# Two padded small tiles, an earlier use of the first weight tile's low parts, and two sums of squares moved to VectorE in a streaming-encoder block

## The chip, the cores and the metric

One core of one Trainium2 chip runs the whole program. The metric is the device time of one execution in microseconds; the kernel before took 2420.36 us (median of 3 runs, 2420.31 to 2421.14).

## What is computed

One layer of a streaming encoder on x of 256 tokens by 2048 features, float32, with norm(x) = x * rsqrt(mean(x*x) + eps) * gain:

```python
x = x + 0.5 * swiglu(norm(x), ffn1_w_up, ffn1_w_down)      # 2048 -> 2 x 5632 -> 2048
proj = norm(x) @ w_in                                      # HGRN2, RG-LRU, gates
merged = g[..., 0, :] * (y_a @ w_branch_a) + g[..., 1, :] * (y_b @ w_branch_b)
x = x + merged @ w_out
x = x + cross_attention(norm(x), norm(mem), wq, wkv, wo)   # 4 heads, 256 memory tokens
x = x + 0.5 * swiglu(norm(x), ffn2_w_up, ffn2_w_down)
return norm(x)                                             # with the final gain
```

## The kernel before, in words

All matrices are float32, and TensorE multiplies in fp32r. Each operand is therefore split: ScalarE copies it to fp32r (its high part, `h` of a weight, `xh` of an activation; L156), and VectorE subtracts that from the original (its low part, `l` or `xl`; L157). A product is the sum of three matmuls: high by high, activation-low by weight-high (both L582), and activation-high by weight-low (L584). The weight is the moving operand, 128 x 512; the activation is the stationary one, 128 x 128.

A weight tile is 128 x 2048, 1 MB, in four quarters of 512 columns. `weights` keeps two tiles ahead of TensorE; `prepare` loads one (SyncE, L290 and others) and splits it. In the two feed-forward layers (`ffn`) a tile of the up-projection meets two operand halves and two token halves. A "plain" tile makes eight products of three matmuls each, 24 matmuls. A "fast" tile makes seven (a Winograd form): it needs sums of its quarters, made by VectorE in `td` (L314 to L317) and split to `th` and `tl`, so its low parts lie in two tiles: three of its seven weight-low matmuls read `l`, four read `tl`. A "mixed" tile uses differences of activations, `xd`, as stationary operands. The tables `FIRST` and `ffn_order` give 70 fast and 10 mixed tiles to the first feed-forward layer (FFN1), 86 and 2 to the second (FFN2). In FFN1, GpSimd's queue also makes some weight-low parts by an accumulating DMA.

Where tiles lie: pools opened for the whole program come first (`const`, `raw` 3 buffers, `h` 3, `l` 3, `slots` 22, then `small`). The pools of a stage (`scope`: `wide`, `xd`, `raw1`, `raw2`, `hd`, `tmp` and others) follow `small`. In the built program every buffer of `raw`, `h`, `l` and `slots` begins at 128 modulo 256 in its partition, and every buffer of a stage's pools at 0 modulo 256 (the first at 185088). `tl` lies in `wide`, a stage's pool. `xd` lies in a stage's pool in FFN1, and in `slots` in FFN2.

At the start, before the first eight tiles are in, the order on SyncE, ScalarE and VectorE is that of the code (`manual_schedule`): tile 0 comes in four quarters, `head_x` loads and splits the activations, and after tiles 4 and 5 `head_residual` loads the residual and adds up its squares for the first norm (`TokenSquares.add`, L468: one ScalarE instruction and a read of its accumulator for each of 4 column blocks c and 2 token halves). The results are first needed where FFN1's first group is activated. `three` writes the matmuls of a tile; TensorE's order is that of the code where the scheduler has no reason to differ.

Of the kernel before, what the change touches and what calls it, by code (L numbers as in the profile page):

```python
# [13 lines left out]
P = 128  # L14
# [80 lines left out]
def block_kernel(ctx: ExitStack, tc: tile.TileContext, xT, xin, memT, vec, gfin, bgate, lruw, wu1, wd1, win, wv,  # L95
# [362 lines left out]
    class TokenSquares:  # L458
# [2 lines left out]
        def __init__(self):  # L461
            self.ss = small.tile([P, 8 + PAD], F32, name="sst", tag="sst")[:, :8]

        def add(self, c, ts=range(2)):
            for t in ts:
                name = "hd" if "hd" in scoped else "tmp2"
                junk = scoped[name].tile([P, 512], F32, name="junk", tag=name)
                act.activation(junk, xt[c][:, t * 512:(t + 1) * 512], ACT.Square,  # L468
                               accum_out=self.ss[:, t * 4 + c:t * 4 + c + 1])

        def rstd_tokens(self, ts=range(2)):
            std = small.tile([P, 2], F32, name="stdt", tag="stdt")
# [99 lines left out]

    held = []

    def three(products, last=0, hold=False, apart=0):


        high = [(acc, ah, bh, start) for acc, (ah, al), (bh, bl), start, _ in products]
        low = [(acc, al, bh, False) for acc, (ah, al), (bh, bl), _, _ in products]
        for i in range(len(high) + apart):  # L580
            for acc, a, b, start in high[i:i + 1] + (low[i - apart:i - apart + 1] if i >= apart else []):
                pe.matmul(acc, a, b, start=start, stop=False)  # L582
        for acc, (ah, al), (bh, bl), _, stop in held + products[last:] + ([] if hold else products[:last]):
            pe.matmul(acc, ah, bl, start=False, stop=stop)  # L584
        held[:] = products[:last] if hold else []
# [13 lines left out]
    def ffn(name, pairs, sq, then, begin=(), sums=()):  # L599
# [38 lines left out]
        for at, e in enumerate(order):  # L638
            w = weights(name, *e)
            kind = e[0]  # L640
            following = order[at + 1][0] if at + 1 < len(order) else None
            if kind != "down":
                g, p = e[1:]
                fast = kind == "fast"
                products = []
                for i, (a, b, n) in enumerate(PRODUCTS["ready" if sums_ready(name, e) else kind]):
                    u = uses[g, n]
                    if u[0] == (p, i):
                        accs[n] = bank()
                    own, less = pairs[p]  # L650
                    products.append((accs[n], part(own, a, P) if a >= 0 else part(less, -1 - a, P), part(w[b // 4] if fast else w, b % 4, 512),
                                     u[0] == (p, i), u[-1] == (p, i)))
                three(products, 3 if adds(name, e) else 0, adds(name, e) and p == 6,
                      2 if at == 0 and name == "ffn1" else 0)
                last = at + 1 == len(order) or order[at + 1][1] != g or following == "down"
                ends = kind != "plain" and uses[g, 0][-1][0] == p
                if ends or last:
                    if ends or kind == "plain":
                        if "hid" in scoped:
                            ev = [scoped[n].tile([P, 1024], F32, name=n, tag=n) for n in ("hid", "hd")]  # L660
                            e0, e3, e1, e2 = (v[:, i:i + 512] for v in ev for i in (0, 512))
                        else:
                            ev = scoped["wide"].tile([P, 2048], F32, name="ev", tag="wide")
                            e0, e1, e2, e3 = (ev[:, i * 512:(i + 1) * 512] for i in range(4))
                        if rstd is None:
                            with tc.issue_after(done["high"]):
                                rstd = sq.rstd_tokens()
                if ends:
                    act.activation(e0, accs[0], ACT.Copy)
                    dve.tensor_tensor(out=e1, in0=accs[5], in1=e0, op=ALU.add)  # L670
                    dve.tensor_tensor(out=e2, in0=accs[4], in1=e1, op=ALU.add)
                if last:
                    if kind == "plain":
                        activate(e0, accs[0], accs[1], 0)
                        activate(e3, accs[3], accs[2], 1)
                    else:
                        for o, n, x in ((e0, 1, e0), (e1, 3, e1), (e1, 2, e1)):
                            dve.tensor_tensor(out=o, in0=accs[n], in1=x, op=ALU.add)
                        activate(e0, e0, e1, 0)
                        for o, n, x in ((e3, 6, e2), (e2, 3, e2)):  # L680
                            dve.tensor_tensor(out=o, in0=accs[n], in1=x, op=ALU.add)
                        activate(e3, e3, e2, 1)
                    late.append((4 if g else 2, lambda g=g, hid=(e0, e3): turn(g, hid)))
            else:
                first, n, c, block = e[1:]
                if block == first:
                    accs["down"] = [bank(), bank()]
                for t in range(2):
                    products = []
                    for k in range(4):  # L690
                        a = hids[2 * block + k // 2][:, k % 2 * 512:][:, :512]
                        products.append((accs["down"][t], (a[:, t * P:][:, :P], a[:, T + t * P:][:, :P]),
                                         part(w, k, 512), block == first and k == 0, block == first + n - 1 and k == 3))
                    three(products)
                    if block == first + n - 1:
                        o = xt[c][:, t * 512:(t + 1) * 512]
                        done["residual"] = dve.scalar_tensor_tensor(out=o, in0=accs["down"][t], scalar=0.5, in1=o,
                                                                    op0=ALU.mult, op1=ALU.add).ins
                        if block == NG - 1:
                            then(c, t)  # L700
            if sums:
                sums.pop(0)()
            if begin:
                begin.pop(0)()
            tick()
# [36 lines left out]
    def head_residual(i):  # L742
        for c in (2 * i, 2 * i + 1):
            for t in range(2):
                sp.dma_start(xt[c][:, t * 512:(t + 1) * 512], xin[t * P:(t + 1) * P, c * 512:(c + 1) * 512])
            sq1.add(c)
        if i:
            sp.dma_start(vt[:, small_n:NVEC], vec[:, small_n:])

# [528 lines left out]
    def to_out(c, t):  # L1278
        if c % 2 == t == 0:
            gains.append(slot(name="gfin"))  # L1280
            sp.dma_start(gains[-1], gfin[:, c * 512:c * 512 + 1024])
        g = gains[c // 2][:, c % 2 * 512:][:, :512]
        sq5.add(c, [t])
        if c == 2:
            b = more.setdefault(t, small.tile([P, 2], F32, name=f"more{t}", tag=f"more{t}"))
            dve.tensor_reduce(out=b[:, :1], in_=sq5.ss[:, 4 * t:4 * t + 3], axis=mybir.AxisListType.X, op=ALU.add)
            dve.tensor_scalar(out=b[:, 1:], in0=b[:, :1], scalar1=1.0 / D, scalar2=EPS, op0=ALU.mult, op1=ALU.add)
        y = [xt[i][:, t * 512:(t + 1) * 512] for i in range(4)]
        if c < 3:
            dve.tensor_tensor(out=y[c], in0=y[c], in1=g, op=ALU.mult)  # L1290
        if c == 2 and t:
            root_ready(y[c])
        if c == 3:
            st = small.tile([P, 2], F32, name="stdt", tag="stdt")
            r = st[:, 1:]
            scaled = slot(name="scaled")[:, :512]
            dve.tensor_tensor(out=scaled, in0=y[3], in1=g, op=ALU.mult)
            act.activation(st[:, :1], sq5.ss[:, 4 * t + 3:4 * t + 4], ACT.Sqrt, bias=more[t][:, 1:], scale=1.0 / D)
            dve.reciprocal(out=r, in_=st[:, :1])
            if t:  # L1300
                with tc.issue_after(done["residual"]):
                    flush(put_off)

            def scale(i, o):
                if i > 1:
                    dve.tensor_scalar(out=o, in0=o, scalar1=r, scalar2=None, op0=ALU.mult)
                else:
                    act.activation(o, o, ACT.Copy, scale=r)
                sp.dma_start(out_[t * P:(t + 1) * P, i * 512:(i + 1) * 512], o)

            for i, o in ((3, scaled), (0, y[0]), (2, y[2]), (1, y[1])):
                if t or i != 2:
                    scale(i, o)
                else:
                    put_off.append(lambda: scale(2, y[2]))
# [101 lines left out]
```

## Time and profile before

| | |
|---|---|
| median of 3 runs | 2420.36 us |
| the profiled execution | 2419.32 us, its span 2417.6 us |
| TensorE matmul busy | 2405.3 us (99%), clock 0.999 |
| VectorE / ScalarE busy | 2048.9 us (85%) / 1467.1 us (61%) |
| DMA | 684.34 MB, mean 283 GB/s |

Rows of the profile give an engine, a line, an operation, the tiles (out<-in), the shape and a count. A row of the timeline begins with its start and its length in microseconds; consecutive instructions of one kind are merged, with their count after the x. The length of a matmul (0.39 us) is not its share of the time: matmuls overlap, and what one costs is the distance from its start to the next one's start, here 0.226 to 0.24 us. FFN1 runs from 6 to about 690 us, FFN2 from about 1735 us to the end.

### The profile page before, as it was taken

To read this page: it belongs to the slowest core of one execution; us is meant where nothing else is said; L and a number is where in the kernel's file an instruction comes from. 1 tells how busy PE (TensorE), PEld (TensorE's weight loads), DVE (VectorE), ACT (ScalarE), POOL (GpSimd) and SP (SyncE) were. 2 spreads that over 40 slices of the span, in tenths; PEclk is the share of its full clock that TensorE was granted. 3 is DMA by queue.
4 is the path that set the end of the run, shared out by engine and by line. 5 is a ranking of instruction groups with operands and counts; after the bars stand their busy time and mean duration, and the time that the engine had idled before them with its cause. 6 is when DMAs were issued, how large, how long until landed. Compare 5 with 4: busy or idle time off the path is not lost.

```text
span 2417.6 us, 30836 instructions
## 1 busy us (share of the span) xinstructions
PE 2405.3 (99%) x12102; PEld 2002.6 (83%) x12102; DVE 2048.9 (85%) x2289; ACT 1467.1 (61%) x1506; POOL 102.3 (4%) x166
## 2 busy tenths in 40 slices
PE   9999999999999999999999999999999999999998
PEld 7888888888888888888888888888888788888887
DVE  7999999999876878688876777777789999999995
ACT  8566777777654454476434555455676666666664
POOL 0000000000000000000000000000000000000000
PEclk9999999999999999999999999999999999999999
DMA  8578999999858776878998899876787878777873
GB/s 306 202 224 257 277 275 274 271 276 276 270 211 316 275 286 247 301 280 315 356 330 338 304 356 337 325 294 239 266 340 304 293 272 288 268 285 275 293 279 142
DMA packets 102386, 684.34 MB, mean 283 GB/s; under 512 B 11360, under 2 KB 11616, under 8 KB 29280
## 3 DMA queue, kind: packets, MB, share of 16 engines
q1 hardware_dynamic: 78912, 519.82, 57.6%
q0 software_dynamic: 23328, 162.54, 22.4%
q8 instruction: 95, 1.56, 0.2%
q14 instruction: 51, 0.42, 0.0%
HBM read 619.40 MB, written 62.91 MB: 282 GB/s over the span
## 4 chain that ended last, share of the span: by engine, by line
PE 96%; ACT 2%; DMA 1%; DVE 1%; issue 0%; SPq 0%; ACTq 0%; DVEq 0%
PE acc L582 35%; PE acc L584 17%; PE acc L342 11%; PE acc L367 8%; PE acc L368 8%; PE acc L370 8%; PE acc L345 6%; ACT h L156 1%; PE acc L622 1%; PE acc L506 1%; DMA raw<-wu 1%; DVE l L157 0%; PE acc L938 0%; DMA raw<-wd 0%; PE acc L1237 0%
## 5 line engine op out<-in xcount | busy, mean ns | idle before, releaser
L156 ACT ACTIVATE h<-raw 128x2048 fp32r<-128x2048 f32 (+3 forms) x577 | 866.8, 1528 | 622.5 <-PE acc L368 211.4
L157 DVE TENSOR_TENSOR l<-raw,h 128x2048 fp32r<-128x2048 f32 (+2 forms) x405 | 833.0, 2059 | 211.4 <-ACT h L156 207.6
L582 PE MATMUL acc<-h,xh 128*128 128x512 f32 x1228 | 478.8, 393 | 2.0 <-ACT h L156 1.1
L582 PE MATMUL acc<-h,xl 128*128 128x512 f32 x1228 | 476.3, 390 | 0.0
L582 PE MATMUL acc<-h,hidop 128*128 128x512 f32 x1408 | 352.8, 391 | 1.4 <-ACT h L156 1.3
L367 PE MATMUL acc<-h,ops 128*128 128x512 f32 x832 | 326.3, 392 | 0.0
L368 PE MATMUL acc<-h,ops 128*128 128x512 f32 x832 | 324.4, 390 | 0.0
L582 PEld LDWEIGHTS acc<-h,hidop 128*128 128x128 f32 x1408 | 262.4, 188 | 56.7 <-ACT h L156 2.5
L582 PEld LDWEIGHTS acc<-h,xh 128*128 128x128 f32 x1228 | 230.3, 188 | 58.9 <-ACT h L156 7.5
L342 PE MATMUL acc<-ops,h 128*128 128x512 f32 x1152 | 277.5, 392 | 0.0
L582 PEld LDWEIGHTS acc<-h,xl 128*128 128x128 f32 x1228 | 230.6, 188 | 48.0
L342 PEld LDWEIGHTS acc<-ops,h 128*128 128x128 f32 x1152 | 211.4, 188 | 41.3
L157 DVE TENSOR_TENSOR tl<-raw,h 128x1024 fp32r<-128x1024 f32 x172 | 203.6, 1218 | 14.6 <-ACT h L156 14.2
L370 PE MATMUL acc<-l,ops 128*128 128x512 f32 x832 | 205.6, 389 | 0.0
L156 ACT ACTIVATE h<-td 128x1024 fp32r<-128x1024 f32 x140 | 146.3, 1055 | 81.6 <-DVE td L314 31.1
L584 PE MATMUL acc<-l,hidop 128*128 128x512 f32 x704 | 190.6, 389 | 0.0
L370 PEld LDWEIGHTS acc<-l,ops 128*128 128x128 f32 x832 | 156.2, 188 | 32.4
L367 PEld LDWEIGHTS acc<-h,ops 128*128 128x128 f32 x832 | 156.2, 188 | 32.1
L368 PEld LDWEIGHTS acc<-h,ops 128*128 128x128 f32 x832 | 156.3, 188 | 31.4
L584 PE MATMUL acc<-tl,xh 128*128 128x512 f32 x624 | 179.9, 394 | 0.0
L157 DVE TENSOR_TENSOR tl<-td,h 128x1024 fp32r<-128x1024 f32 x140 | 169.9, 1218 | 8.9 <-ACT h L156 7.9
L584 PE MATMUL acc<-l,xh 128*128 128x512 f32 x604 | 166.9, 390 | 0.0
(254 smaller groups left out, 2481.6 us busy)
## 6 DMA issues: line engine op xcount, KB each, us to landing
raw<-wu SPq DMA_DIRECT2D x114, 1024.0 KB, 6.1
raw<-wd SPq DMA_DIRECT2D x88, 1024.0 KB, 6.7
prep<-wu POOLq DMA_DIRECT2D x58, 1024.0 KB, 6.9
t<-prep POOLq DMA_DIRECT2D x58, 1024.0 KB, 5.4
raw<-t SPq DMA_DIRECT2D x58, 1024.0 KB, 7.1
raw<-wu SPq DMA_DIRECT2D x58, 768.0 KB, 5.1
raw<-win SPq DMA_DIRECT2D x40, 1024.0 KB, 4.9
raw<-wg SPq DMA_DIRECT2D x32, 1024.0 KB, 5.3
```

The lines of the kernel that those rows point to most:

```text
L156: done["high"] = act.activation(h, raw, ACT.Copy).ins
L157: done["low"] = dve.tensor_tensor(out=l, in0=raw, in1=h.bitcast(F32), op=ALU.subtract).ins
L342: pe.matmul(acc, h[:, k * P:(k + 1) * P], xs[k], start=k == 0, stop=False)
L345: done["product"] = pe.matmul(acc[:, :T], l[:, k * P:(k + 1) * P], xs[k][:, :T], start=False, stop=k == KT - 1).ins
L367: pe.matmul(accs[t], x[:, t * P:][:, :P], h[j], start=first and j == 0, stop=False)
L368: pe.matmul(accs[t], x[:, T + t * P:][:, :P], h[j], start=False, stop=False)
L370: done["product"] = pe.matmul(accs[t], x[:, t * P:][:, :P], l[j], start=False, stop=last and j == 3).ins
L506: pe.transpose(acc[:, z * T + t * P:][:, :P], tile[:, t * 512 + (2 * y + z) * P:][:, :P], ident)
L582: pe.matmul(acc, a, b, start=start, stop=False)
L584: pe.matmul(acc, ah, bl, start=False, stop=stop)
L622: pe.transpose(acc[:, z * T + t * P:][:, :P], hid[t][:, (2 * y + z) * P:][:, :P], ident)
```

## The change

Three edits. Two tiles `more0` and `more1` of the last norm, two buffers each, grow from 2 to 16 floats; they take 64 bytes instead of 32 each, `small` grows by 128 bytes, and every buffer of every stage's pool moves up by 128 (the first to 185216, which is 128 modulo 256). In the first tile, `three` issues the weight-low matmuls of the first two quarters right behind their other matmuls. In `head_residual` the squares of the last column block (c = 3) are a VectorE multiply and a VectorE reduction instead of ScalarE's.

```diff
-        def add(self, c, ts=range(2)):
+        def add(self, c, ts=range(2), by_vector=False):
...
+                x, o = xt[c][:, t * 512:(t + 1) * 512], self.ss[:, t * 4 + c:t * 4 + c + 1]
+                if by_vector:
+                    dve.tensor_tensor(out=junk, in0=x, in1=x, op=ALU.mult)
+                    dve.tensor_reduce(out=o, in_=junk, axis=mybir.AxisListType.X, op=ALU.add)
+                else:
+                    act.activation(junk, x, ACT.Square, accum_out=o)
...
-    def three(products, last=0, hold=False, apart=0):
+    def three(products, last=0, hold=False, early=0):
...
+        if early:
+            for i in range(0, len(high), 2):
+                for acc, a, b, start in high[i:i + 2] + low[i:i + 2]:
+                    pe.matmul(acc, a, b, start=start, stop=False)
+                if i < early:
+                    for acc, (ah, _), (_, bl), _, _ in products[i:i + 2]:
+                        pe.matmul(acc, ah, bl, start=False, stop=False)
+            high, low, products = [], [], products[early:]
...
-                      2 if at == 0 and name == "ffn1" else 0)
+                      4 if at == 0 and name == "ffn1" else 0)
...
-            sq1.add(c)
+            sq1.add(c, by_vector=c == 3)
...
-            b = more.setdefault(t, small.tile([P, 2], F32, name=f"more{t}", tag=f"more{t}"))
+            b = more.setdefault(t, small.tile([P, PAD], F32, name=f"more{t}", tag=f"more{t}")[:, :2])
```

TensorE, tile 0, the first matmuls behind the warm-up, before (224 to 227 are four accumulators; 224 and 225 take the first and third quarter, 226 and 227 the second and fourth; `h_183` and `l_184` are the tile's parts):

```order
L582 MATMUL acc_224<-h_183,xh_178 128x512
L582 MATMUL acc_225<-h_183,xh_178 128x512
L582 MATMUL acc_224<-h_183,xl_179 128x512
L582 MATMUL acc_225<-h_183,xl_179 128x512
L582 MATMUL acc_226<-h_183,xh_178 128x512
L582 MATMUL acc_227<-h_183,xh_178 128x512
L582 MATMUL acc_226<-h_183,xl_179 128x512
L582 MATMUL acc_227<-h_183,xl_179 128x512
```

The same place on TensorE in the change:

```order
L587 MATMUL acc_224<-h_183,xh_178 128x512
L587 MATMUL acc_225<-h_183,xh_178 128x512
L587 MATMUL acc_224<-h_183,xl_179 128x512
L587 MATMUL acc_225<-h_183,xl_179 128x512
L587 MATMUL acc_226<-h_183,xh_178 128x512
L587 MATMUL acc_227<-h_183,xh_178 128x512
L590 MATMUL acc_224<-l_184,xh_178 128x512
L590 MATMUL acc_225<-l_184,xh_178 128x512
L587 MATMUL acc_226<-h_183,xl_179 128x512
L587 MATMUL acc_227<-h_183,xl_179 128x512
L590 MATMUL acc_226<-l_184,xh_178 128x512
L590 MATMUL acc_227<-l_184,xh_178 128x512
```

Four weight-low matmuls (L590) move from the tile's end to between the second quarter's matmuls; the first of them stands behind the second quarter's first two, not ahead of them.

VectorE, around tiles 5 and 6, before (`l<-raw` are the low parts of tiles 5 and 6, `xl<-xg` those of activations 6 and 7, `stdt` the sum of the squares):

```order
L157 TENSOR_TENSOR l<-raw,h 128x2048
L476 TENSOR_REDUCE stdt<-sst 128x2
L157 TENSOR_TENSOR xl<-xg,xh 128x512
L157 TENSOR_TENSOR l<-raw,h 128x2048
L157 TENSOR_TENSOR xl<-xg,xh 128x512
```

The same place on VectorE in the change (`x_98` is column block 3 of the residual):

```order
L157 TENSOR_TENSOR l<-raw,h 128x2048
L470 TENSOR_TENSOR junk<-x_98 128x512
L471 TENSOR_REDUCE sst<-junk 128x1
L470 TENSOR_TENSOR junk<-x_98 128x512
L471 TENSOR_REDUCE sst<-junk 128x1
L157 TENSOR_TENSOR xl<-xg,xh 128x512
L480 TENSOR_REDUCE stdt<-sst 128x2
L157 TENSOR_TENSOR l<-raw,h 128x2048
```

Four instructions come in ahead of activation 6's low part, and `stdt` moves behind that part. On ScalarE two of the four squares between the high parts of tiles 5 and 6 are gone. Everywhere else the five engines' orders are the same but for line numbers.

More of the change, by code (lines that the diff above doesn't have):

```diff
@@ L467, in add @@
                 junk = scoped[name].tile([P, 512], F32, name="junk", tag=name)
-                act.activation(junk, xt[c][:, t * 512:(t + 1) * 512], ACT.Square,
-                               accum_out=self.ss[:, t * 4 + c:t * 4 + c + 1])
+                x, o = xt[c][:, t * 512:(t + 1) * 512], self.ss[:, t * 4 + c:t * 4 + c + 1]
[4 more added lines that the diff above has]
+                    act.activation(junk, x, ACT.Square, accum_out=o)
         def rstd_tokens(self, ts=range(2)):
@@ L573, in block_kernel @@
     held = []
-    def three(products, last=0, hold=False, apart=0):
+    def three(products, last=0, hold=False, early=0):
         high = [(acc, ah, bh, start) for acc, (ah, al), (bh, bl), start, _ in products]
         low = [(acc, al, bh, False) for acc, (ah, al), (bh, bl), _, _ in products]
-        for i in range(len(high) + apart):
-            for acc, a, b, start in high[i:i + 1] + (low[i - apart:i - apart + 1] if i >= apart else []):
-                pe.matmul(acc, a, b, start=start, stop=False)
+        if early:
[6 more added lines that the diff above has]
+            high, low, products = [], [], products[early:]
+        for acc, a, b, start in [m for pair in zip(high, low) for m in pair]:
+            pe.matmul(acc, a, b, start=start, stop=False)
         for acc, (ah, al), (bh, bl), _, stop in held + products[last:] + ([] if hold else products[:last]):
```

## Prediction

> **What bounds the kernel now.** I read first the busy times and the chain of work that ended last, then the busy times by stretch, then the timeline at the places that the change touches.
>
> ```profile
> PE 2405.3 (99%) x12102; PEld 2002.6 (83%) x12102; DVE 2048.9 (85%) x2289; ACT 1467.1 (61%) x1506; POOL 102.3 (4%) x166
> PE 96%; ACT 2%; DMA 1%; DVE 1%; issue 0%; SPq 0%; ACTq 0%; DVEq 0%
> 480.00:520.00 40.00, 40.00 (x176) 32.38 (x175) 39.93 (x41) 29.22 (x24) 2.62 (x3) 1.00 0.92 280
> 2020.00:2060.00 40.00, 40.00 (x181) 32.90 (x180) 36.63 (x37) 24.67 (x22) 0.88 (x1) 1.00 0.87 298
> ```
>
> TensorE sets the time: 96% of the chain, at full clock. So time can go in two ways only: a shorter distance from matmul to matmul, or a wait of TensorE's that vanishes. The third row (columns: stretch, its length, PE, PEld, DVE, ACT, POOL, clock, DMA share, GB/s) shows a second fact: in FFN1 VectorE is as full as TensorE, 39.93 of 40 us. In FFN2 it has 3.4 of 40 us free.
>
> **The opening: low parts used by quarters.** The rows of tile 0:
>
> ```profile
> 6.48 0.62 PE L582 MATMUL acc<-h,xl 128*128 128x512 f32 x2
> 7.52 0.73 PE L582 MATMUL acc<-h,xh 128*128 128x512 f32 x2 [0.41 <-ACT h L156]
> 8.09 0.62 PE L582 MATMUL acc<-h,xl 128*128 128x512 f32 x2
> 6.50 0.68 DVE L297 TENSOR_TENSOR l<-raw,h 128x512 fp32r<-128x512 f32 x1
> 7.50 2.04 DVE L157 TENSOR_TENSOR l<-raw,h 128x512 fp32r<-128x512 f32 x3 [0.32 <-ACT h L156]
> 6.83 1.98 ACT L156 ACTIVATE h<-raw 128x512 fp32r<-128x512 f32 x3 [1.21 <-DMA raw<-wu]
> ```
>
> From 6.48 two matmuls fill 0.46 us, to 6.94; the next starts at 7.52. These 0.58 us are a wait for the second quarter's high part, which ScalarE starts at 6.83, when its DMA lands. The first quarter's low part is ready at 6.50 + 0.68 = 7.18 and could use the gap from there, but in the change its matmuls stand behind the second quarter's first two, and TensorE keeps its order. So the wait stays. The low part of the second quarter is ready a third of 2.04 us after 7.50, at 8.2, and is needed six matmuls after 7.52, at 9.0. The later quarters are needed 0.9 us later than before, when ScalarE has long made them (6.83 + 1.98 = 8.81). I cost this edit at **nothing**. It can lose nothing, since every operand is in earlier than its new turn; it can gain at most 7.52 - 7.18 = 0.34 us, if the wait were filled after all.
>
> **The squares.** The rows around tile 6:
>
> ```profile
> 37.58 1.98 PE L584 MATMUL acc<-l,xh 128*128 128x512 f32 x8
> 39.83 0.50 PE L582 MATMUL acc<-h,xh 128*128 128x512 f32 x1 [0.27 <-ACT h L156]
> 40.17 0.40 PE L582 MATMUL acc<-h,xl 128*128 128x512 f32 x1
> 35.02 0.63 ACT L468 ACTIVATE junk<-x 128x512 f32<-128x512 f32 x1
> 36.41 0.90 ACT L530 ACTIVATE xg<-xf 128x256 f32<-128x256 f32 x2
> 37.88 1.90 ACT L156 ACTIVATE h<-raw 128x2048 fp32r<-128x2048 f32 x1
> 29.03 0.33 SPq L290 DMA_DIRECT2D raw<-wu  x1
> raw<-wu SPq DMA_DIRECT2D x1, 1024.0 KB, 6.2
> 33.66 2.29 DVE L157 TENSOR_TENSOR l<-raw,h 128x2048 fp32r<-128x2048 f32 x1 [1.12 <-DMA raw<-wu]
> 38.01 0.69 DVE L157 TENSOR_TENSOR xl<-xg,xh 128x512 fp32r<-128x512 f32 x1 [1.31 <-ACT xh L156]
> 36.54 0.16 DVE L476 TENSOR_REDUCE stdt<-sst 128x2 f32<-128x8 f32 x1 [0.58 <-ACT junk L468]
> L1195 DVE TENSOR_REDUCE st<-p 128x1 f32<-128x256 f32 x8 | 3.3, 416 | 0.2
> ```
>
> Eight matmuls of 0.227 us from 37.58 end at 39.40, but the next starts at 39.83, and the one behind it 0.34 instead of 0.23 us later: 0.43 + 0.11 = 0.54 us of waiting for ScalarE's high part of tile 6 (37.88 + 1.90 = 39.78). Column block 3's squares hold ScalarE from 35.02 to 36.41. Without them the high part is done 1.39 us sooner, at 38.39, a microsecond before its turn. The tile's DMA doesn't stop that: it is issued at 29.03 and lands 6.2 us later, at 35.2.
>
> What comes next to be late is VectorE. It ends tile 5's low part at 33.66 + 2.29 = 35.95 and then makes two squares and two reductions ahead of activation 6's low part (the block itself is in: ScalarE read it at 35.02 without a wait). A square is as long as the 0.69 us of `xl`, which has the same shape. No row shows a reduction of 512: 256 elements take 0.42 us and 2 take 0.16, so the slope gives 0.68; the ends are 0.42 and twice that, 0.83. With 0.68 the four end at 35.95 + 2 x 0.69 + 2 x 0.68 = 38.69 and `xl` at 39.38. TensorE's second matmul of the tile wants it at 39.40 + 0.23 = 39.63: 0.25 us to spare. With 0.42 there is 0.77 to spare, with 0.83 it is 0.05 late. I take the whole gain, **0.54 us**, with 0.49 as the lower end. VectorE had idle time here (the bracketed 1.31, 0.58 and more), so tile 6's low part isn't later than before.
>
> **The offsets.** This edit touches no instruction, but every buffer of a stage's pools. First the cost of a mismatch, for `tl` in FFN1 and FFN2, then for `xd` in FFN1 and FFN2:
>
> ```profile
> 407.96 0.84 PE L584 MATMUL acc<-l,xh 128*128 128x512 f32 x3
> 408.64 1.09 PE L584 MATMUL acc<-tl,xh 128*128 128x512 f32 x4
> 409.56 0.39 PE L582 MATMUL acc<-h,xh 128*128 128x512 f32 x1
> 2134.41 0.84 PE L584 MATMUL acc<-l,xh 128*128 128x512 f32 x3
> 2135.09 1.09 PE L584 MATMUL acc<-tl,xh 128*128 128x512 f32 x4
> 2136.02 0.39 PE L582 MATMUL acc<-h,xh 128*128 128x512 f32 x1
> 106.84 1.10 PE L582 MATMUL acc<-h,xd 128*128 128x512 f32 x4
> 107.78 1.07 PE L584 MATMUL acc<-l,xh 128*128 128x512 f32 x4
> 1768.99 1.07 PE L582 MATMUL acc<-h,xd 128*128 128x512 f32 x4
> 1769.89 1.29 PE L584 MATMUL acc<-l,xh 128*128 128x512 f32 x5
> L584 PE MATMUL acc<-tl,xh 128*128 128x512 f32 x624 | 179.9, 394 | 0.0
> ```
>
> Both operands at 128 modulo 256 (`l`): 0.68 / 3 = 226.7 ns a matmul, twice. `tl` at 0 against `xh` at 128: 0.92 / 4 = 230 and 0.93 / 4 = 232.5, mean 231.2, so 4.5 ns more. `xd` is the cleanest sign, the same matmul in both places: 0.94 / 4 = 235 ns where it lies in a stage's pool, 0.90 / 4 = 225 where it lies in `slots`. Since the rows are rounded to 0.01 us I take 8 ns.
>
> The whole of it: 624 x 4.5 = 2.8 us for `tl`, of which the 280 in FFN1 (70 fast tiles) are 1.26 and the 344 in FFN2 1.55; and 60 matmuls with `xd` in FFN1 (10 mixed tiles by 6) x 8 ns = 0.48. Together 3.3 us, if 128 against 128 always costs what it costs in these rows.
>
> Not all of it arrives. In FFN1 TensorE runs into VectorE:
>
> ```profile
> 422.45 1.21 DVE L157 TENSOR_TENSOR tl<-td,h 128x1024 fp32r<-128x1024 f32 x1
> 423.72 0.73 PE L584 MATMUL acc<-tl,xh 128*128 128x512 f32 x2
> 424.29 0.39 PE L582 MATMUL acc<-h,xl 128*128 128x512 f32 x1
> 1911.19 0.74 PE L584 MATMUL acc<-tl,xh 128*128 128x512 f32 x2
> 1913.22 0.96 PE L582 MATMUL acc<-h,hidop 128*128 128x512 f32 x3 [1.29 <-ACT h L156]
> ```
>
> The `tl` that TensorE reads at 423.72 was written until 423.66, and the two matmuls take 0.57 instead of 0.46: 0.11 us of waiting. What TensorE saves ahead of such a place is lost there; what it saves behind it stays, because it frees buffers earlier, and VectorE starts the next tiles earlier. I take half of FFN1's `tl`, 0.6, and 0.4 of `xd`'s 0.48, which falls mostly into the first 150 us. In FFN2 there is one large wait, 1911.19 to 1913.22 (2.03 us for 0.46 us of work), which swallows what was saved since the chain that ends there began; I take 1.2 of 1.55. The offsets so bring **2.2 us**, between 0 and 3.3.
>
> The Trainium skill, in "TensorE: Matmul & The Clock Gate", section "Step-by-step: what each phase is for", says that TensorE reads the moving operand and the next weights through two independent SBUF ports, so that loading weights takes nothing from the running matmul. By that rule the offset of one against the other would bring 0 instead of 2.2. The 235 against 225 ns of `xd` speak against it.
>
> **The sum.** 0 + 0.54 + 2.2 = 2.7 us. The profiled execution took 2419.32 us, 1.7 us around a span of 2417.6; less 2.7 it is 2416.6. The median of the runs is 1.04 us above the profiled execution, so I predict 2420.36 - 2.7, rounded to **2417.6 us**, 0.11% less. About 0.2%, 4.84 us, is what a measurement of this kernel can tell from no change.
>
> **The rivals.**
>
> *The offset isn't the cause.* The slow matmuls share more than an offset: `tl` and `xd` are fresh from VectorE, and lie higher in the memory. Then padding brings nothing and the squares alone count: 2420.36 - 0.54 = 2419.8 us. For it: after the move no pair lies as the quick ones do; by the addresses the new distance is 256 modulo 512, which no row of before has. Against it: `xd` in FFN2 is just as fresh, and quick. The skill's rule above would give this time too.
>
> *All of it arrives, and FFN2's stall eases.* The wait before 1913.22 ends a chain through ScalarE and transfers. With VectorE less late, most of its 1.57 lost us (2.03 - 0.46) could go, say 1.4: 2420.36 - 0.54 - 3.3 - 1.4 = 2415.1 us. For it: nothing in FFN2 is full but TensorE. Against it: the chain starts from buffers that TensorE frees, so both ends move together.
>
> *The new distance is worse (slower).* Pairs 256 apart could collide more than pairs 128 apart. The worst pair in this trace:
>
> ```profile
> 169.27 0.64 PE L582 MATMUL acc<-h,xd 128*128 128x512 f32 x2
> 169.75 0.62 PE L584 MATMUL acc<-tl,xh 128*128 128x512 f32 x2
> ```
>
> 0.48 / 2 = 240 ns. At that pitch the 624 lose 8.8 ns each, 5.5 us, and the 60 some 5 ns, 0.3: 2420.36 + 5.8 - 0.54 = 2425.6 us; nothing hides it, since TensorE is the bound. It decides from 239 ns on for a loss over 4.84 us, and from 232 on for any loss. For it: no row excludes it. Against it: within the quick pairs the distance changes by multiples of 512 without such a price.
>
> **How the numbers follow.** The forecast 0.56 (its own range 2416.3 to 2419), the offset without effect 0.13, all of it with the stall 0.24, the worse distance 0.07. Faster by over 0.2% (below 2415.5) is the third case alone, 0.24; slower by over 0.2% the fourth, 0.07; within it the first two, 0.69. The range has to leave out no more than 0.2: I let go the fourth case and the far half of the third, and put its low end at 2414.8 and its high end at 2420.8, a microsecond above the squares alone, since runs of one kernel differ by 0.8 here.
>
> **What would show it.** Right, if in the profile after: `tl` runs of four take 0.91 us like `l`'s, and `xd` in FFN1 0.90; the wait ahead of tile 6 is gone while the 0.58 us in tile 0 stay; VectorE's reduction is near 0.68; and part of FFN1's gain turns up as waits for `tl`. Wrong, if `tl` stays at 231 ns or rises, if activation 6's low part comes late, or if the waits around 1913 change by more than the matmuls do.

## The result, and the profile after

| | before | after |
|---|---|---|
| median, 22 runs each | 2420.58 us (2418.14 to 2422.56) | 2416.93 us (2415.26 to 2421.68) |
| ratio | | 0.9986, 95% interval 0.998 to 0.9993 |
| the profiled execution | 2419.32 us | 2416.49 us |
| its span | 2417.6 us | 2414.7 us |

The changed kernel is 3.65 us faster, 0.15%: less than the 0.2% that the prediction took as what a measurement can tell, though the interval of the ratio lies below 1, and 0.7 us below the forecast of 2417.6. The sum came out, but the gain in pitch (the distance from matmul to matmul) was forecast too small and the waits that it brings as well, and the two made up for each other in part; the sections below take them apart. First the page of the profile after: its busy times and its chain, and one stretch of FFN1 (columns as before).

```profile
PE 2400.2 (99%) x12102; PEld 2003.2 (83%) x12102; DVE 2051.1 (85%) x2293; ACT 1466.9 (61%) x1502; POOL 102.3 (4%) x166
PE 98%; DMA 1%; ACT 1%; DVE 0%; issue 0%; SPq 0%; ACTq 0%; DVEq 0%
480.00:520.00 40.00, 40.00 (x180) 32.45 (x179) 39.60 (x41) 29.70 (x25) 2.62 (x3) 1.00 0.93 295
```

The same 12102 matmuls are busy for 5.1 us less. TensorE carries 98% of the chain instead of 96. VectorE is still full in FFN1, 39.60 of 40 us.

The opening. The wait for the second quarter's high part is still there, and the low part stands behind the second quarter's first two matmuls, as the order said:

```profile
5.97 0.61 PE L587 MATMUL acc<-h,xl 128*128 128x512 f32 x2
7.51 0.73 PE L587 MATMUL acc<-h,xh 128*128 128x512 f32 x2 [0.93 <-ACT h L156]
8.09 0.62 PE L590 MATMUL acc<-l,xh 128*128 128x512 f32 x2
6.00 0.68 DVE L297 TENSOR_TENSOR l<-raw,h 128x512 fp32r<-128x512 f32 x1
6.83 2.01 ACT L156 ACTIVATE h<-raw 128x512 fp32r<-128x512 f32 x3 [1.71 <-DMA raw<-wu]
```

TensorE ran dry at 5.97 + 0.46 = 6.43 and went on at 7.51. The first quarter's low part was ready at 6.00 + 0.68 = 6.68, and nothing used it until 8.09. Tile 1 starts within 0.02 us of where it started before (12.18 against 12.20).

The squares. TensorE, VectorE and ScalarE around tile 6:

```profile
37.58 1.98 PE L595 MATMUL acc<-l,xh 128*128 128x512 f32 x8
39.39 0.40 PE L593 MATMUL acc<-h,xh 128*128 128x512 f32 x1
39.63 0.40 PE L593 MATMUL acc<-h,xl 128*128 128x512 f32 x1
36.63 0.69 DVE L471 TENSOR_REDUCE sst<-junk 128x1 f32<-128x512 f32 x1
38.08 0.69 DVE L471 TENSOR_REDUCE sst<-junk 128x1 f32<-128x512 f32 x1
38.68 0.68 DVE L157 TENSOR_TENSOR xl<-xg,xh 128x512 fp32r<-128x512 f32 x1
36.41 1.90 ACT L156 ACTIVATE h<-raw 128x2048 fp32r<-128x2048 f32 x1
```

The eight matmuls are followed by the next at 39.39, without the 0.43 + 0.11 us of before. The high part is done at 38.31, and activation 6's low part at 39.36 for a turn at 39.63. The reduction takes 0.69 us where 0.68 was estimated.

The offsets. A run with `tl` in FFN1, one in FFN2, and one with `xd` in FFN1:

```profile
405.93 0.84 PE L595 MATMUL acc<-l,xh 128*128 128x512 f32 x3
406.61 1.07 PE L595 MATMUL acc<-tl,xh 128*128 128x512 f32 x4
407.52 0.39 PE L593 MATMUL acc<-h,xh 128*128 128x512 f32 x1
2133.36 1.07 PE L595 MATMUL acc<-tl,xh 128*128 128x512 f32 x4
2134.26 0.39 PE L593 MATMUL acc<-h,xh 128*128 128x512 f32 x1
105.75 1.07 PE L593 MATMUL acc<-h,xd 128*128 128x512 f32 x4
106.65 1.52 PE L595 MATMUL acc<-l,xh 128*128 128x512 f32 x6
```

From start to start: 0.91 and 0.90 us for four `tl`, 0.90 for four `xd`; before it was 0.92, 0.93 and 0.94. So the steps that the prediction wanted to see are there. What they brought in all can be worked out, because the kernels issue the same matmuls: I set each one's distance to the next in the one trace against the same one's in the other. Distances more than 33 ns above the usual 227 count as waits, the rest as pitch. In microseconds:

| stretch of the kernel before | shorter pitch | waits before | waits after |
|---|---|---|---|
| 45 to 150 | 1.13 | 0.41 | 0.44 |
| 150 to 690 (rest of FFN1) | 1.94 | 2.45 | 3.80 |
| 1730 to 1870 (FFN2 begins) | 0.69 | 0.64 | 0.62 |
| 1870 to 1925 | 0.24 | 3.31 | 4.73 |
| 1925 to the end | 2.09 | 1.92 | 2.88 |

Between 690 and 1730 us both change by 0.05 us at most. Together 6.1 us of pitch, and in this execution 3.7 us of new waits that take more than half of it back. The prediction had 3.3 and 1.1.

### The profile page after: what moved, and what is told of

Its sections match the earlier page's. It is cut to its first block, busy times and chain, and to the rows that moved or that the text cites. A ratio compares the mean times of both kernels' runs of the same rounds, so it can differ in the third digit from the quotient of the medians.

```text
span 2414.7 us, 30834 instructions
## 1 busy us (share of the span) xinstructions
PE 2400.2 (99%) x12102; PEld 2003.2 (83%) x12102; DVE 2051.1 (85%) x2293; ACT 1466.9 (61%) x1502; POOL 102.3 (4%) x166
## 4 chain that ended last, share of the span: by engine, by line
PE 98%; DMA 1%; ACT 1%; DVE 0%; issue 0%; SPq 0%; ACTq 0%; DVEq 0%
PE acc L593 36%; PE acc L595 18%; PE acc L342 11%; PE acc L367 8%; PE acc L368 8%; PE acc L370 8%; PE acc L345 6%; PE acc L633 1%; PE acc L510 1%; DMA raw<-wu 1%; ACT h L156 0%; PE acc L949 0%; PE acc L1248 0%; PE acc L1202 0%; DMA raw<-t 0%; PE acc L1064 0%
```

## The experiments

The theory after the traces: the padding brings 6 us of pitch, more than predicted since matmuls behind a mismatched one were slow as well, and 3 to 4 us of it are given back, in FFN1 to VectorE and in FFN2 to transfers. Rivals: the gain comes from the other two edits, or the waits come from elsewhere. Every time is a median of 10 or 11 runs (one run for each of the two repeats at the end); the ratio is to the kernel before on the same chip, with its 95% interval.

### Each edit by itself

Padding alone:

```diff
-            b = more.setdefault(t, small.tile([P, 2], F32, name=f"more{t}", tag=f"more{t}"))
+            b = more.setdefault(t, small.tile([P, PAD], F32, name=f"more{t}", tag=f"more{t}")[:, :2])
```

> The kernel before with only the two tiles padded. My theory: the common offset makes every mismatched matmul and its neighbours faster, some 6 us in all by the two traces, and waits behind it take back about 3.7, so this kernel is 2.3 us faster than the kernel before (2418.3). In its profile the runs of four with tl take 0.91 us in both layers. Rival: the squares and the first tile's new order are what eased the chain, and the padding alone is absorbed: within 0.5 us of the kernel before, with tl still near 227 ns but as much more waiting.

Measured: 2416.89 us, ratio 0.9985 (0.9977 to 0.9994). The padding alone gives the whole gain of the change as far as the runs can tell, 3.7 us where 2.3 were expected; the rival is out. In its profile the pitch is 1.11, 1.91, 0.69, 0.25 and 1.99 us shorter in the five stretches. The execution also has one wait of 1.53 us for a low part that no other profile shows:

```profile
636.42 1.97 PE L582 MATMUL acc<-h,hidop 128*128 128x512 f32 x8
639.76 1.20 PE L584 MATMUL acc<-l,hidop 128*128 128x512 f32 x4 [1.37 <-DVE l L157]
```

Eight matmuls of 0.227 end at 638.24, and the next starts at 639.76. One wait of this size in one execution is nearly half of what the change is worth, so the profile of one execution can't weigh a term of half a microsecond by its span; the matched distances can.

The squares alone, with the new `add` and

```diff
-            sq1.add(c)
+            sq1.add(c, by_vector=c == 3)
```

> The kernel before with only the squares of column block 3 on VectorE. My theory: the wait ahead of tile 6 goes, 0.54 us, and stays gone at the end: 0.5 us faster. Rival: FFN1's full VectorE takes it back, so the wait ahead of tile 6 is gone in the profile but the time is that of the kernel before, 0.0.

Measured: 2420.84 us, ratio 0.9998 (0.999 to 1.0007): no gain to be seen, and 0.5 us is inside the interval. In the trace the wait ahead of tile 6 is gone, and TensorE is 0.37 us ahead of the kernel before at 61 us, counted from the start, or 0.44 counted from tile 1. At 242 us it still has 0.27; then it loses 0.37 in one place:

```profile
257.86 1.99 PE L586 MATMUL acc<-h,hidop 128*128 128x512 f32 x8
259.95 0.50 PE L586 MATMUL acc<-h,xh 128*128 128x512 f32 x1
260.29 0.39 PE L586 MATMUL acc<-h,xl 128*128 128x512 f32 x1
```

The eight should end at 259.67, and the matmul at 259.95 is again 0.11 too long. The trace's list of waits names ScalarE's high part, and behind it a transfer. One other profile has a wait of TensorE's ahead of the same matmul, that of the kernel with a difference of 64 (below), 0.93 us:

```profile
259.78 0.50 PE L593 MATMUL acc<-h,xh 128*128 128x512 f32 x1 [0.77 <-ACT h L156]
```

There ScalarE waits for VectorE's sums. These two are the only kernels that have the squares on VectorE and operands that don't lie alike; with the padding the wait isn't there. Whether the squares bring it on, one execution of each can't tell, so the rival is neither shown nor excluded. What is shown: 0.54 us at 39 us, and a time at the end that doesn't tell 0.5 from 0.

The first tile's order alone, with the new `three` and `4 if at == 0` for `2 if at == 0`:

> The kernel before with only the new order of the first tile. My theory: 0.0, since the wait for the second quarter's high part stays in front of the moved matmuls, and every later quarter is in time either way. Rival: the moved matmuls fill what the trace shows between the second quarter's arrival and its low part, up to 0.34 us faster.

Measured: 2420.24 us, ratio 1.0 (0.999 to 1.0009): nothing, as expected. Its profiled execution is 1.8 us late at tile 1, which isn't the order's doing; it returns at the end of this document.

TensorE held to the order of the code, on top of the whole change:

```diff
-                in_turn.enter_context(tc.manual_schedule(engines={sp.engine, act.engine, dve.engine}))
+                in_turn.enter_context(tc.manual_schedule(engines={sp.engine, act.engine, dve.engine, pe.engine}))
```

> The changed kernel, with TensorE held to the order of the code in the first eight tiles: the first quarter's two weight-low matmuls then stand ahead of the second quarter's first two. My theory: in the changed kernel's trace the first quarter's low part is ready at 6.68, TensorE stands idle from 6.43 to 7.51; two matmuls fit between, so tile 1 starts 0.45 us earlier and the time is 0.45 us under the changed kernel's. Rival: the next thing to be late (tile 1's first quarter, or the wait ahead of a later tile) takes it: the 0.45 us show in tile 0 and are gone by 60 us.

```profile
6.25 0.62 PE L587 MATMUL acc<-h,xl 128*128 128x512 f32 x2
7.01 0.73 PE L590 MATMUL acc<-l,xh 128*128 128x512 f32 x2
7.58 0.63 PE L587 MATMUL acc<-h,xh 128*128 128x512 f32 x2
```

Two weight-low matmuls now stand where TensorE waited. Tile 1 starts at 11.71 instead of 12.18; 0.07 of this 0.47 us is an earlier landing (ScalarE starts the second quarter at 6.76 instead of 6.83). Between 30 and 39 us some 0.16 of it is lost, as the rival had it, and 0.31 are left at 815 us. Measured: 2416.30 us, ratio 0.9984 (0.9975 to 0.9992), 0.6 us under the changed kernel; the two intervals overlap. It is the fastest of the versions that compute all of it, and it is what the edit to the first tile needed: the matmuls written in a new order only, the scheduler put them behind the wait.

### What counts about an offset

The other pools moved instead, `raw`, `h`, `l` and `slots` to 0 modulo 256, where the stage's pools lie in the kernel before (`const` grows by 128 bytes and `small` shrinks by 128):

```diff
-    par = const.tile([P, 96], F32, name="par")
+    par = const.tile([P, 96 + 32], F32, name="par")
...
-            self.ss = small.tile([P, 8 + PAD], F32, name="sst", tag="sst")[:, :8]
+            self.ss = small.tile([P, 8], F32, name="sst", tag="sst")
```

> The kernel before, with the stage pools left at 0 modulo 256 and all the others (raw, h, l, slots) moved by 128 to 0 modulo 256 instead. My theory: what counts is that the two operands of a matmul lie alike, not where: runs of four with tl take 0.91 us and xd in FFN1 0.90, those with l stay at 0.91, and the time is that of the kernel with padding alone, 2416.9. Rival: offset 0 is itself the slow place, then tl stays at 0.92 to 0.93 and the matmuls with l and h fall to it too, 10 us slower and more.

```profile
406.57 0.84 PE L584 MATMUL acc<-l,xh 128*128 128x512 f32 x3
407.25 1.07 PE L584 MATMUL acc<-tl,xh 128*128 128x512 f32 x4
408.16 0.39 PE L582 MATMUL acc<-h,xh 128*128 128x512 f32 x1
106.31 1.07 PE L582 MATMUL acc<-h,xd 128*128 128x512 f32 x4
107.22 1.07 PE L584 MATMUL acc<-l,xh 128*128 128x512 f32 x4
```

All runs of four take 0.91 us, `l` stays at 0.68 / 3, and the time is 2417.03 us, ratio 0.9989 (0.998 to 0.9997). So the place itself doesn't matter, nor where in memory `tl` and `xd` lie or who wrote them: they stayed where they were. That settles the first rival of the prediction. In this kernel `tl` and its `xh` lie a multiple of 512 apart, in the changed one 256 apart modulo 512, and the pitch is the same, which settles the third.

One of the two tiles padded, so that the stage's pools lie at 64 modulo 256 and the others at 128:

```diff
-            b = more.setdefault(t, small.tile([P, PAD], F32, name=f"more{t}", tag=f"more{t}")[:, :2])
+            b = more.setdefault(t, small.tile([P, PAD if t else 2], F32, name=f"more{t}", tag=f"more{t}")[:, :2])
```

> The changed kernel with one of the two tiles padded, so that the stage pools lie at 64 modulo 256 and the others at 128. My theory: any difference modulo 256 costs as much as 128 does, so tl's runs of four take 0.92 to 0.93 us again, the two matmuls behind them are slow again, and the time is about 2420, the kernel before less the squares. Rival: only a difference of 128 costs, 64 is free: 0.91 us, and the time is 2416.9.

```profile
408.69 1.09 PE L595 MATMUL acc<-tl,xh 128*128 128x512 f32 x4
409.62 0.39 PE L593 MATMUL acc<-h,xh 128*128 128x512 f32 x1
105.86 1.08 PE L593 MATMUL acc<-h,xd 128*128 128x512 f32 x4
106.78 1.53 PE L595 MATMUL acc<-l,xh 128*128 128x512 f32 x6
```

A difference of 64 costs too, though not the same: `tl` 0.93 / 4, over its runs of four in FFN2 233.3 ns (231.2 at a difference of 128), `xd` 0.92 / 4 = 230 (235 before). 2420.18 us, ratio 1.0002 (0.9993 to 1.001). The theory holds in direction; "as much as 128" is wrong by a few nanoseconds both ways.

How far a mismatch reaches is seen best in the means over the 67 undisturbed runs of four `tl` in FFN2 that are followed by four matmuls with `h`, in ns from start to start, worked out from the traces. The operands of the four behind lie alike in all three kernels:

| | ahead | tl 1 | 2 | 3 | 4 | behind 1 | 2 | 3 | 4 |
|---|---|---|---|---|---|---|---|---|---|
| before | 226.7 | 234.0 | 224.5 | 237.1 | 229.2 | 231.8 | 232.4 | 231.0 | 226.9 |
| after | 226.9 | 226.7 | 227.0 | 226.7 | 226.7 | 227.0 | 226.7 | 226.7 | 226.8 |
| at 64 | 226.7 | 233.2 | 233.3 | 233.3 | 233.3 | 226.0 | 235.7 | 228.4 | 232.5 |

Before, three matmuls behind the run were slow as well: 32.6 ns a run from first to last instead of the 18 that the four alone cost in the prediction. By groups of matched matmuls, before against after: 2.2 us from `tl`, 0.5 from `xd`, 1.9 from the two matmuls behind either, 0.8 from the third behind, and 0.7 spread over some 4500 others, where two kernels without padding (the one before and the squares alone) differ by 0.3 as well.

### Who takes it back in FFN1

The kernel before with less work for VectorE in FFN1, the fourth sum left out and the raw quarter split in its place:

```diff
-            dve.tensor_tensor(out=td[:, 1536:], in0=raw[:, 1536:], in1=td[:, 1024:1536], op=ALU.subtract)
+            if "raw1" not in scoped:
+                dve.tensor_tensor(out=td[:, 1536:], in0=raw[:, 1536:], in1=td[:, 1024:1536], op=ALU.subtract)
...
-            split(th[:, a:a + 1024], tl[:, a:a + 1024], td[:, a:a + 1024])
+            split(th[:, a:a + 1024], tl[:, a:a + 1024], (raw if a and "raw1" in scoped else td)[:, a:a + 1024])
```

> The kernel before with less work for VectorE in FFN1: the fourth of the four sums of a fast tile is left out there, and its low part is made of the raw quarter instead, 0.6 to 0.7 us less for each of 70 tiles. My theory: VectorE has some 45 us to spare then, so the waits for tl at 301.16, 423.72 and 546.28 go; FFN1 has few other waits, so the time falls by 0.3 to 1.5 us only. Rival: those waits come from transfers, and stay.

> The same with the padding as well. My theory: in the three kernels with padding the waits between 150 and 690 us grow by 1.3 us, at the same places in every group of 61 us, because VectorE has no time to keep up with a faster TensorE. With VectorE relieved they don't, so against the relieved kernel without padding the padding gains 1.8 to 1.9 us between 150 and 690 instead of 0.6. Rival: the waits come from ScalarE or from transfers, then the gain there stays 0.6.

Measured: 2424.47 us without padding, ratio 1.0018 (1.0009 to 1.0027), and 2416.26 with it, 0.9985 (0.9976 to 0.9994). Both expectations missed. Less work made the kernel slower: `raw` is held until the later split (SyncE's loads now wait for VectorE's `tl`, where they waited for the fourth sum), and new waits of up to 1.80 us for `l` come up once in each group of 61 us. The padding is worth 8.2 us here, 4.1 of it between 150 and 690 us, where the waits fall from 7.58 to 5.42 us. That is no answer to the question, because the relief made a bound of its own; why padding shortens that one was not followed up.

The relief without that bound, the third sum's part split twice:

```diff
+            if a and "raw1" in scoped:
+                v = [w[:, 1024:].rearrange("p (i n) -> p i n", i=2) for w in (th, tl)]
+                split(*v, td[:, None, 1024:1536].broadcast_to([P, 2, 512]))
+                continue
```

> The kernel before with less work for VectorE in FFN1 once more, now without holding the raw tiles longer: the fourth sum of a fast tile is left out, and the third sum's part is split into high and low parts twice in its place. My theory: VectorE has some 45 us to spare in FFN1, and the waits for tl at 301, 424 and 546 us go, so the time is 0.3 to 1.5 us under the kernel before. Rival: other waits come up as with the version that held the raw tiles longer, and the time rises by 1 us or more.

> The same with the padding. My theory: VectorE's full load is what takes back 1.3 us of the padding between 150 and 690 us; relieved, it takes back nothing, and against the relieved kernel without padding TensorE gains 1.8 to 1.9 us there instead of 0.4 to 0.6. Rival: the waits there come from buffers or transfers, then the gain stays at 0.4 to 0.6.

The stretch from 61 to 650 us in the kernel before (columns as above):

```profile
61.00:650.00 589.00, 589.00 (x2616) 481.29 (x2615) 573.99 (x598) 414.53 (x348) 33.27 (x38) 1.00 0.85 261
```

The same stretch in the relieved kernel:

```profile
61.00:650.00 589.00, 589.00 (x2624) 485.08 (x2623) 536.62 (x529) 411.76 (x348) 33.30 (x38) 1.00 0.85 262
```

And in the relieved kernel with padding:

```profile
61.00:650.00 589.00, 588.95 (x2634) 486.42 (x2633) 538.76 (x531) 412.31 (x348) 33.30 (x38) 1.00 0.85 262
```

VectorE, the third busy time, has 37 us less to do, and the three waits for `tl` are gone from the trace. Measured: 2418.73 us without padding, ratio 0.9994 (0.9985 to 1.0003, which doesn't tell the forecast gain from none), and 2414.37 with it, 0.9976 (0.9967 to 0.9985): the padding is worth 4.4 us. Between 150 and 690 us TensorE gains 1.59 of 2.10 us of shorter pitch, somewhat less than the 1.8 to 1.9 expected; with a full VectorE it gained 0.59 of 1.94. So VectorE's load is what took back most of FFN1's gain: the new waits there fall from 1.35 to 0.51 us. Its mark in the changed kernel is a wait of two parts, here at one of its places, with the last `tl` that VectorE wrote for it:

```profile
421.35 0.39 PE L593 MATMUL acc<-h,xh 128*128 128x512 f32 x1
421.70 0.74 PE L595 MATMUL acc<-tl,xh 128*128 128x512 f32 x2
422.28 0.40 PE L593 MATMUL acc<-h,xl 128*128 128x512 f32 x1
420.42 1.22 DVE L157 TENSOR_TENSOR tl<-td,h 128x1024 fp32r<-128x1024 f32 x1
```

0.35 us from the first to `tl` and 0.58 for the two, instead of 0.23 and 0.45. The `tl` is written until 421.64, and VectorE has worked without a wait since 405.46. The mark stands at 298.9, 421.35 and 543.8 us, 122.5 us or two of FFN1's groups apart; smaller waits lie between, at 360.6, 483.1 and 605.6 us among others.

### Who takes it back in FFN2

The changed kernel twice more:

> The changed kernel once more, unchanged, for one more profile. My theory: the 1.2 us that the stretch from 1870 to 1925 us lost in its first profile come from a transfer of raw that took 8.35 us there and took between 6.86 and 7.99 in the other profiles, whatever the kernel; so the stretch varies from profile to profile of one and the same kernel by 0.5 us or more, in step with that transfer. Rival: the changed kernel always meets the slow transfer; 8.35 and 4.7 us of waits come back within 0.1.

> As the run before, one more profile of the changed kernel: by my theory the waits from 1870 to 1925 us differ from those of the other two profiles by some tenths and go with the transfer's length; by the rival they are 4.7 again. The regular waits in FFN1 (some 3.7 to 3.8 us between 150 and 690) should come back in both.

In the chain of waits one transfer ends shortly before 1890 us, and ScalarE's high part starts when it lands (a row is its start, its length, and what it is). In the first profile of the changed kernel:

```profile
1879.70 8.35 DMA raw<-wu
```

In the first repeat:

```profile
1880.34 7.17 DMA raw<-wu
```

In the second:

```profile
1879.45 7.07 DMA raw<-wu
```

With 8.35, 7.17 and 7.07 us for the one transfer the waits from 1870 to 1925 us are 4.73, 3.58 and 3.20. The code of FFN2 is the same in all versions here, but for the offsets: those whose operands don't lie alike have 6.86 to 7.76 us and waits of 3.0 to 4.1 (five profiles; a sixth, in which the clock fell at this place, is told of at the end), those whose operands do have 6.96 to 8.35 us and waits of 3.2 to 4.9 (eight profiles). A straight line through these thirteen gives 1.2 us more of waits for each microsecond of the transfer, and at the same transfer 0.15 us more with operands alike. So the 1.42 us that this stretch lost in the first profile was for the most part that execution's transfer, and not a constant of the change. From 1925 us on the waits are 2.0 to 3.6 with operands alike, 1.7 to 2.4 without (means 2.7 and 2.0); there too they move by a microsecond within one kernel (2.88, 2.34 and 3.43 for the changed one). That a shorter pitch lengthens the waits of FFN2 by some tenths on the mean is likely, and not settled. FFN1's waits came back at 3.89 and 3.78 us, 3.80 in the first profile.

## Why the prediction was right, and where it wasn't

**The opening: right.** Nothing, by the trace (0.02 us) and by the run of that edit alone. The gap it left is worth 0.4 us at tile 1 when TensorE's order is held, a little above the 0.34 that the prediction put as the most: in that execution the first quarter's low part was in at 6.96 instead of 7.18.

**The squares: the mechanism right to the hundredth, the last step not shown.** The wait of 0.54 us went, with the reduction at 0.69 and `xl` at 39.36 (39.38 forecast). That it would arrive at the end was argued with VectorE's idle time around tile 6. The runs can't tell: nothing alone, within some 2 us either way, a new wait of 0.37 us in the one profile, and 2416.93 with all edits against 2416.89 for padding alone.

**The offsets: the cause right, the size too small.** "624 x 4.5 = 2.8 us" looked at four matmuls of a run and took the rows behind it for the undisturbed pitch. `tl` itself gave 2.2, a fifth less, and `xd` 0.5 as forecast; but the three matmuls behind gave another 2.7, and 0.7 came from the rest. Raw 6.1 instead of 3.3. The trace of before had it, some rows further. Behind the `tl` of FFN2 that the prediction quotes, matmuls with `h` go on at 2136.02, and the fifth behind that one is this row:

```profile
2137.17 0.39 PE L582 MATMUL acc<-h,xl 128*128 128x512 f32 x1
```

1.15 / 5 = 230 ns a matmul, where 226.7 is usual.

The Trainium skill ("TensorE: Matmul & The Clock Gate", section "Step-by-step: what each phase is for") has the two operands come in over two ports that don't disturb each other. The times at three relative offsets don't fit that: 226.8 ns alike, 231.2 at 128 apart, 233.3 at 64 apart. Why the offset counts, no run here shows.

**What doesn't arrive: the mechanism right in FFN1, its price too low everywhere.** Of FFN1's 1.74 us the prediction gave up 0.74 to VectorE. The runs showed 1.3 to 1.4 given back of 3.1, nearly the same share of a larger gain, and 0.5 when VectorE was relieved. In FFN2 it gave up 0.35 to the large wait at 1911 to 1913. There the first profile gave back 1.4 between 1870 and 1925 us and 1.0 behind, the first repeat 0.3 and 0.4, the second -0.1 and 1.5. Pitch less new waits is so 2.4 us in the first profile, 3.9 and 3.1 in the repeats. So the padding's part was 2.2 in the sum and measured 3.7 alone (1.5 to 5.6 by the interval), close to its far end of 3.3. That the sum came so near is in part luck: a gain forecast at half its size (3.3 of 6.1) was met by a loss forecast at half its size or less (1.1 of 2.1 to 3.7). Had I carried the right pitch with the absorption as I had put it, a third, I would have forecast 4 us for it and been right for a better reason.

**The rivals.** The offset without effect and the worse distance fell by the padding alone and by the pools moved the other way. "All of it arrives and FFN2's stall eases" fell too: the stall eases and grows with a transfer that the change doesn't touch.

**What the prediction named as signs** came as named, but one: it counted it as wrong if the waits around 1913 changed by more than the matmuls do. They did, by 1.4 against 0.24, and the repeats show that this sign was badly chosen: it moves by as much between two executions of one program.

## What to carry to other kernels

When a stream of matmuls has the same shape everywhere, compare the distances from start to start between groups of one kernel by the addresses of their operands, and look some matmuls past the group: here 128 bytes of padding were worth 3.7 us (1.5 to 5.6), and the removal of a wait in plain sight half a microsecond at most. Price a faster engine by what runs full beside it: with slack there, the same padding brought a microsecond more in FFN1. And a wait that ends in a transfer is measured on several executions before anything is put down to the change.

## What else the runs showed

A stop of 2.1 us was followed by half the clock. In the relieved kernel that holds `raw` longer TensorE stood idle before 1897.13; from 1898.6 on it ran at half speed for 3 us:

```profile
1897.13 0.50 PE L583 MATMUL acc<-h,xh 128*128 128x512 f32 x1 [2.10 <-ACT h L156]
1900.29 0.63 PE L583 MATMUL acc<-h,xh 128*128 128x512 f32 x1
1900.71 0.63 PE L583 MATMUL acc<-h,xl 128*128 128x512 f32 x1
```
```profile
1898.60:1901.60 3.00, 3.00 (x9) 2.31 (x8) 3.00 (x4) 2.39 (x3) 0.00 (x0) 0.51 0.56 164
```

0.42 us from matmul to matmul at a granted clock of 0.51: eight matmuls lost 0.2 us each, 1.6 us. The Trainium skill ("TensorE: Matmul & The Clock Gate", section "Why this matters for your kernels") puts the limit at about 3 us without work. Here, if the stop is the reason, less was enough once. From start to start the stop is 2.49 us; one of 2.03 us at 309.94 in the same trace left the clock alone, and so did the longest of the changed kernel, 2.00 us at 1887.69. One case doesn't show that the stop is the reason, nor where the limit lies.

The opening has slow matmuls as well, of a cause that stays open. In the profile of the new order alone, the one that was 1.8 us late at tile 1, they are slow until 10.8 us (the last row is the stretch, its columns as before):

```profile
8.24 1.22 PE L583 MATMUL acc<-h,xh 128*128 128x512 f32 x2 [0.30 <-ACT h L156]
9.26 1.05 PE L586 MATMUL acc<-l,xh 128*128 128x512 f32 x2
10.11 0.86 PE L583 MATMUL acc<-h,xl 128*128 128x512 f32 x2
10.81 0.62 PE L586 MATMUL acc<-l,xh 128*128 128x512 f32 x2
8.20:10.80 2.60, 2.56 (x6) 2.05 (x7) 2.01 (x3) 2.56 (x6) 0.00 (x0) 1.00 1.01 370
```

From 8.24 on two matmuls take 1.02, 0.85 and 0.70 us instead of the 0.58, 0.46 and 0.46 of the changed kernel: 1.1 us. The other 0.7 us are a later landing (ScalarE's second quarter starts at 7.55 instead of 6.83). The granted clock reads 1.00 in this stretch, so that it is the clock, as above, isn't shown. The second repeat of the changed kernel has one slow pair too, its first (0.99 us from 5.62), and the first repeat has none: it differs between executions of one kernel, and in this one it was worth more than two of the three edits.
